# One decoder step on one core: the samples' top-256 as eight rows halved on ScalarE, and six steps beside it

## The chip, the core and the metric

The kernel runs on one core of one Trainium2 chip. The metric is device time in microseconds (us) of one execution, lower is better. TensorE multiplies matrices, VectorE, ScalarE and GpSimd do the elementwise work, SyncE and two others start DMAs. In rows of the trace PE is TensorE's matmul, PEld its weight load, DVE VectorE, ACT ScalarE, POOL GpSimd.

## What is computed

One layer of a hybrid decoder for 1024 prompt tokens and 8 sample tokens, each sample with 1024 cached positions. The reference, cut to what matters here:

```python
score = jnp.einsum('bqh,bqhl->bql', wi, jax.nn.relu(jnp.einsum('bqhd,bld->bqhl', qi, ki)))
score = jnp.where(causal[None], score, -jnp.inf)
_, sel = lax.top_k(score, topk)            # topk = 256
# attention of the 8 heads over the selected keys and values only
a_out = sparse_attention(...) * silu(ga)
# means over windows of 2, 4, 8, 16 tokens, in four groups of 128 channels
d_g = (cs[t + 1] - cs[t + 1 - w]) / min(pos + 1, w) - u
p_out = (d_g @ w_pool[g]) * pool_scale * silu(gp)
y = x + gate * (concat(a_out, p_out) @ w_out)
```

For a prompt token the 256 largest scores are taken among its causal positions; for a sample among its 1024 cached positions and itself.

## The kernel before

Work stands in this order: the input is transposed and normed (to about 64 us), then come projections in chunks of 344 columns, each a sum of three matmuls for each of eight slices of the inner dimension (`products`, fp32 split in an upper and a lower part). The first eight projections (`first_order`: k, qi1, ga0, qi2, ga1, qi3, ga2, v) run beside the indexer of the prompt; the next thirteen (`order`: u0, u1, u2, gp0, u3, gp1, q0, gp2, q1, q2, q3, gp3, ga3) beside all that the change touches; then come attention and the output projection.

The order on TensorE, VectorE and ScalarE is that of the program (`manual_schedule`), so an instruction that waits holds all that stands behind it on its engine. Side work is written as generators in named queues: `beside(queue, gen, rate)` adds one, `project` calls `tick` after every second slice (six matmuls, four times a chunk, twelve times a projection), and a tick advances the head of each queue by `rate` steps, a step being what lies between two `yield`s. `lag(n)` is n empty steps. `drain` runs what is left. Queues: `weights` (loads and splits of the coming projections' weights), `prep`, `score`, `pool`, `win`, `smp`, `top`, `gate`, `stack`.

What the change touches:

- `topk` (L740, queue `top`, rate TOP = 0.5): the 256 largest of each row for the six prompt blocks TB = 7, 6, 5, 4, 3, 2, 128 tokens each, on 128 partitions. Eight halvings of a threshold `t`: the scores under it are counted, by ScalarE (Sign with an accumulator, L759) for blocks 7, 6 and 5, by VectorE (L762) for the others, and VectorE moves all six thresholds (L765 to L769). Then two rounds of MAX8 and MATCH_REPLACE8 (`largest` L793, `mark` L800) pick the last up to 16 of each row exactly. If any row needs more, which a matmul counts (`p_bad`, `tk_bad`), a branch runs thirty more rounds. Last come the masks `amask` (L829).
- `sample_indexer` (L868, queue `smp`, rate 1) gives the samples' scores `s_sc`, 128 partitions x 9 x 8 samples. `sample_topk` (L937, the same queue) searches the 256th score of each sample bit by bit: twice six rounds (`search`), each comparing 504 candidates on VectorE (`s_fl`, L969) and counting over partitions on TensorE (nine matmuls with `ones_b`, `p_cnt`, L955), then the ties by rank (`p_rk`), then the mask `s_m`.
- `windows` (queue `win`): GpSimd's sums over tokens (L1197), VectorE's means (L1203 to L1208), three empty steps (WLAG), ScalarE's upper part `pdh` (L1211), GpSimd's lower part `pdl` (L1213). `take_gp` multiplies these (`ppo`, L1221) and GpSimd multiplies by the gate (L1226).
- `norm_k` (L1025, queue `prep`, beside the first eight projections): after the sum of squares, one empty step between GpSimd's power and the rest on VectorE (L243).
- The first of the thirteen projections, `u0`, takes its PSUM banks from a pool that opens when the indexer's banks are free; `ps_small` is a pool of two banks that `values` (`pvt`) and `history` (`p_hT`) use too.
- `row` takes one of 29 buffers of 1032 fp32 on 128 partitions.

Of the kernel before, what the change touches and what calls it, by code (L numbers as in the profile page):

```python
# [21 lines left out]
TOP = 0.5  # L22
# [5 lines left out]
WLAG = 3  # L28
# [3 lines left out]
LAG = 5  # L32
# [34 lines left out]
def kernel(  # L67
# [634 lines left out]
    def ordered_halves(hi, lo, src, sign):  # L702
        v = src.bitcast(I16).rearrange("p (n t) -> p n t", t=2)
        nc.vector.tensor_copy(hi, v[:, :, 1])
        nc.vector.tensor_copy(lo, v[:, :, 0].bitcast(U16))
        yield
        nc.vector.tensor_scalar(sign, hi, 0.0, -1.0, op0=ALU.is_lt, op1=ALU.mult)
        nc.vector.tensor_tensor(lo, lo, sign.bitcast(U16), op=ALU.bitwise_xor)
        yield
        nc.vector.scalar_tensor_tensor(hi, sign, 0x7FFF, hi, op0=ALU.bitwise_and, op1=ALU.bitwise_xor)  # L710

    TB = (7, 6, 5, 4, 3, 2)
    BY_ACT = (7, 6, 5)
    NT = len(TB)
# [12 lines left out]
    tk_flag = const.tile([P, NT], BF16, name="tk_flag")  # L727
    for i, b in enumerate(TB):
# [7 lines left out]
    def width(i):  # L736
        return (TB[i] + 1) * P

    def topk():
# [13 lines left out]
        nc.vector.tensor_tensor(t, t, tk_mv[:, :, 0], op=ALU.add)  # L753
        for k in range(HALVINGS):
# [12 lines left out]
            nc.vector.scalar_tensor_tensor(tk["d"], tk["keep"], 0.5 if k < HALVINGS - 1 else 0.0, tk_step[:, k],  # L767
                                           op0=ALU.subtract, op1=ALU.mult)
            nc.vector.tensor_tensor(t, t, tk["d"], op=ALU.add)  # L769
            yield  # L770
        for i, b in enumerate(TB):
# [8 lines left out]
            yield  # L780
# [22 lines left out]
        yield  # L803
        for r in range(WINDOW // 8):
            for i in range(NT):
                largest(i)
                yield
            if r == 0:
                pb = ps_side("p_bad", (P, NT))
                mm(pb, ones_b, tk_flag, start=True, stop=True)  # L810
            those(r)
            if r == 0:
                yield
                with nc.allow_low_precision(reason="a count of at most 768"):
# [50 lines left out]

    def s_bc(t):
        return t.unsqueeze(1).to_broadcast([P, 9, B])

    def sample_indexer():
# [54 lines left out]
        def weigh(b):  # L924
# [842 lines left out]
```

## Time and profile before

| | us |
|---|---|
| median of 3 runs (634.39 to 635.96) | 635.41 |
| profiled execution | 634.29 |
| its span, first to last instruction | 632.6 |

| engine | busy us | share of the span | instructions |
|---|---|---|---|
| PE (TensorE matmul) | 603.4 | 95% | 4197 |
| DVE (VectorE) | 391.7 | 62% | 946 |
| ACT (ScalarE) | 292.0 | 46% | 522 |
| POOL (GpSimd) | 237.7 | 38% | 205 |

The thirteen projections stand between 182.8 and 378 us. A row of the trace's timeline reads: start in us, duration, engine, line, operation, output and inputs, tile and type, count, and in brackets the idle time of that engine before it with what ended it. A releaser is inferred from semaphores; the last of several is named. TensorE's matmuls overlap, so their distance from start to start is the time that each costs.

### The profile page before, as it was taken

To read this page: it belongs to the slowest core of one execution; us is meant where nothing else is said; L and a number is where in the kernel's file an instruction comes from. 1 tells how busy PE (TensorE), PEld (TensorE's weight loads), DVE (VectorE), ACT (ScalarE), POOL (GpSimd) and SP (SyncE) were. 2 spreads that over 40 slices of the span, in tenths; PEclk is the share of its full clock that TensorE was granted. 3 is DMA by queue.
4 is the path that set the end of the run, shared out by engine and by line. 5 is a ranking of instruction groups with operands and counts; after the bars stand their busy time and mean duration, and the time that the engine had idled before them with its cause. 6 is when DMAs were issued, how large, how long until landed. Compare 5 with 4: busy or idle time off the path is not lost.

```text
span 632.6 us, 10965 instructions
## 1 busy us (share of the span) xinstructions
PE 603.4 (95%) x4197; PEld 497.7 (79%) x4197; DVE 391.7 (62%) x946; ACT 292.0 (46%) x522; POOL 237.7 (38%) x205
## 2 busy tenths in 40 slices
PE   6899989999989998799999999999999999999997
PEld 5678989999979888789988876566676566878876
DVE  5887365647464788998765337655686765464242
ACT  6635435545456883223223448755787554202000
POOL 3302343211247559674544782502445033106000
PEclk9899998999999999899999999999999999999999
DMA  9994114130427122122543254311221046056232
GB/s 309 286 284 96 51 34 131 46 93 11 122 56 210 50 67 57 48 68 46 133 121 106 88 154 132 127 35 34 68 68 33 2 132 219 19 169 204 96 101 68
DMA packets 75292, 66.05 MB, mean 104 GB/s; under 512 B 21828, under 2 KB 63900, under 8 KB 75229
## 3 DMA queue, kind: packets, MB, share of 16 engines
q1 hardware_dynamic: 69731, 50.57, 28.3%
q0 software_dynamic: 3008, 10.49, 5.6%
q10 hardware_dynamic: 2498, 4.27, 1.8%
q8 instruction: 33, 0.54, 0.4%
q14 instruction: 22, 0.18, 0.1%
HBM read 54.44 MB, written 11.10 MB: 104 GB/s over the span
## 4 chain that ended last, share of the span: by engine, by line
PE 70%; DVE 10%; ACT 5%; SPq 4%; POOL 3%; issue 3%; DMA 3%; POOLq 0%; ACTq 0%; DVEq 0%
PE py L1700 14%; PE po L1616 7%; PE pj_q L515 7%; PE pT L1600 6%; PE pj_ga L515 6%; PE pl L1579 6%; PE pj_gp L515 4%; PE pi L669 4%; PE pj_qi L515 3%; ACT sg L759 3%; SPq L328 2%; PE pj_k L515 2%; PE pj_v L515 2%; SPq L281 2%; DVE sc L779 1%
## 5 line engine op out<-in xcount | busy, mean ns | idle before, releaser
L678 DVE SCALAR_TENSOR_TENSOR sc<-r,wtok,sc 128x512 f32<-128x512 f32 (+5 forms) x42 | 45.1, 1082 | 28.1 <-ACT r L671 26.9
L1588 ACT ACTIVATE pr<-pr,mx,rq 128x128 f32<-128x128 f32 (+7 forms) x64 | 55.4, 866 | 12.3 <-DVE mx L1586 11.8
L671 ACT ACTIVATE r<-pi 128x512 f32<-128x512 f32 (+5 forms) x48 | 36.3, 760 | 53.4 <-PE pi L669 40.7
L1616 PE MATMUL po<-pTs,v_sb 128*64 128x256 f32 (+1 forms) x320 | 52.6, 381 | 0.0
L1700 PE MATMUL py<-woh,mh 128*128 128x512 f32 (+1 forms) x136 | 52.2, 384 | 0.0
L1700 PE MATMUL py<-woh,ml 128*128 128x512 f32 (+1 forms) x136 | 51.8, 381 | 0.0
L1700 PE MATMUL py<-wol,mh 128*128 128x512 f32 (+1 forms) x136 | 51.8, 381 | 0.0
L1600 PE MATMUL pT<-ident,pr 128*128 128x128 f32 x288 | 48.8, 282 | 0.1
L1582 DVE CUSTOM_DVE_ANT_0 pr<-pl,amask 128x384 f32<-128x384 f32 (+5 forms) x48 | 42.1, 885 | 9.3 <-PE pl L1579 8.9
L1600 PEld LDWEIGHTS pT<-ident,pr 128*128 128x128 f32 x288 | 32.5, 141 | 17.5 <-issue 15.6
L146 ACT COPY pTs<-pT 128x512 f32<-128x512 f32 x40 | 23.3, 582 | 33.5 <-PE pT L1600 33.5
L1720 DVE TENSOR_TENSOR y<-py,gate_p 128x512 f32<-128x512 f32 (+1 forms) x17 | 11.2, 657 | 42.6 <-PE py L1700 42.6
L515 PE MATMUL pj_u<-hh,wh_u 128*128 128x344 f32 x96 | 32.3, 337 | 1.7 <-ACT r L671 1.7
L1444 POOL TENSOR_TENSOR wol<-wo,woh 128x1024 fp32r<-128x1024 f32 x8 | 19.5, 2454 | 36.5 <-ACT woh L1443 30.2
L515 PE MATMUL pj_gp<-hh,wh_gp 128*128 128x344 f32 x96 | 33.1, 345 | 0.0
L148 DVE COPY pTs<-pT 128x512 f32<-128x512 f32 (+1 forms) x40 | 23.3, 582 | 15.0 <-PE pT L1600 12.3
L515 PE MATMUL pj_q<-hh,wh_q 128*128 128x344 f32 x96 | 32.2, 335 | 0.0
L515 PE MATMUL pj_ga<-hh,wh_ga 128*128 128x344 f32 x96 | 31.7, 330 | 0.0
L1616 PEld LDWEIGHTS po<-pTs,v_sb 128*64 128x64 f32 x320 | 18.0, 135 | 17.4 <-issue 9.4
L515 PE MATMUL pj_gp<-hl,wh_gp 128*128 128x344 f32 x96 | 31.5, 329 | 0.0
L515 PE MATMUL pj_gp<-hh,wl_gp 128*128 128x344 f32 x96 | 31.4, 327 | 0.0
L515 PE MATMUL pj_ga<-hh,wl_ga 128*128 128x344 f32 x96 | 31.3, 326 | 0.0
(451 smaller groups left out, 1747.5 us busy)
## 6 DMA issues: line engine op xcount, KB each, us to landing
ada<-in_w_ada_dram SPq DMA_DIRECT2D x16, 512.0 KB
x<-in_x_prompt_dram SPq DMA_DIRECT2D x8, 512.0 KB
gate<-in_w_ada_dram SPq DMA_DIRECT2D x8, 512.0 KB
mix<-mix_dram SPq DMA_DIRECT2D x8, 512.0 KB
xr<-in_x_prompt_dram SPq DMA_DIRECT2D x15, 256.0 KB
out_dram<-y ACTq DMA_DIRECT2D x15, 256.0 KB
mix_dram<-sga SPq DMA_DIRECT2D x12, 172.0 KB
mix_dram<-sgp SPq DMA_DIRECT2D x12, 172.0 KB
```

Source lines behind the costliest of these rows:

```text
L146: nc.scalar.copy(out, in_)
L148: nc.vector.tensor_copy(out, in_)
L515: mm(pt[:m, :n], wt[:, k, :m], ht[k][:, c0:c0 + n], start=k == 0 and q == 0, stop=k == KT - 1 and q == 2)
L669: mm(pt[:, c, :n], lhs, kk[:, l0:l0 + n], start=kk is kih, stop=kk is kil)
L671: nc.scalar.activation(r[:, 0:L].rearrange("p (c n) -> p c n", c=nh), pt[:, 0:nh, :n], AF.Relu)
L678: nc.vector.scalar_tensor_tensor(sb[:, 0:L], r[:, 0:L], wtok[:, b, h:h + 1], sb[:, 0:L], op0=ALU.mult, op1=ALU.add)
L1579: mm(pt[:, c, :n], qst[j][s][:, b * P:(b + 1) * P], ksst[s][w][:, l0:l0 + n], start=w == 0, stop=w == 1)
L1582: nc.vector.tensor_tensor_reduce(out=pr[:, 0:L].rearrange("p (c n) -> p c n", c=nh), in0=pt[:, 0:nh, :n], in1=amask[b].rearrange("p (c n) ...
L1588: exps.append(lambda: nc.scalar.activation(pr[:, 0:L], pr[:, 0:L], AF.Exp, scale=sc, bias=mx, accum_out=sums[j, m][:, bq, s:s + 1]))
L1600: nc.tensor.transpose(pt[:, s, bq * P:(bq + 1) * P], probs[j, 2 * m + bq, s][:, k * P:(k + 1) * P], ident)
L1616: mm(po[j, m][64 * s:64 * s + 64, 0, q0:], v_sb[:, k, 64 * s:64 * s + 64], pTs[j, m, k][:, s, q0:], start=k == 0, stop=k == nk - 1)
L1700: mm(pt[:, part], a[k][:, bs], w[:, part], start=k == ks[0] and q == 0, stop=k == ks[-1] and q == 2)
```

## The change

The samples' search is rewritten. The scores of the eight samples are transposed into eight rows of 1025 on eight partitions (`s_row`), and a threshold per row is halved eight times wholly on ScalarE (`half_way`: Sign over the row with the count accumulated, Sign of the limit minus the count, Identity that moves the threshold by a step). Two rounds on VectorE pick the last up to 16, and `sample_masks` transposes the mask back. The six steps beside it: blocks 7 and 6 of the prompt are halved wholly on ScalarE too, and block 5's count goes to VectorE, so that VectorE moves its own four thresholds alone; the steps of `topk` are cut otherwise and run at TOP = 0.57; `topk` waits before its last rounds until the queue `smp` is empty, and the branch serves both; `norm_k` leaves three empty steps in place of one; the means' upper part on ScalarE comes after six empty steps in place of three; `u0` takes its banks from `ps_small`.

```diff
-TOP = 0.5
+TOP = 0.57
-    BY_ACT = (7, 6, 5)
-    NT = len(TB)
+    BY_ACT = (7, 6)
+    NT, NA = len(TB), len(BY_ACT)
...
+    def half_way(sc, t, cnt, lim, sign, step, junk):
+        nc.scalar.activation(junk, sc, AF.Sign, scale=-1.0, bias=t, accum_out=cnt)
+        nc.scalar.activation(sign, cnt, AF.Sign, scale=-1.0, bias=lim)
+        nc.scalar.activation(t, sign, AF.Identity, scale=step, bias=t)
     def topk():
...
+        for k in range(HALVINGS):
+            nc.gpsimd.tensor_scalar(tk_step[:, k, 0:NA], tk_step[:, k, 0:NA], 0.5, None, op0=ALU.mult)
         yield from lag(2)
...
         for k in range(HALVINGS):
-            for i, b in enumerate(TB):
-                L = width(i)
-                if b in BY_ACT:
-                    nc.scalar.activation(junk_tile("sg", tag="junka", bufs=1)[:, :L], score[b], AF.Sign, scale=-1.0,
-                                         bias=t[:, i:i + 1], accum_out=cnt[:, i:i + 1])
-                else:
-                    nc.vector.tensor_scalar(junk_tile("junk")[:, :L], score[b], t[:, i:i + 1], None,
-                                            op0=ALU.is_lt, op1=ALU.add, accum_out=cnt[:, i:i + 1])
-            yield
-            nc.vector.tensor_tensor(tk["keep"], cnt, tk["least"], op=ALU.is_le)
...
+            for i in range(max(NA, NT - NA)):
+                if i < NA:
+                    half_way(score[TB[i]], t[:, i:i + 1], cnt[:, i:i + 1], tk_lim[:, i:i + 1], tk_sign[:, i:i + 1],
+                             tk_step[:, k, i:i + 1], junk_tile("sg", tag="junka", bufs=1)[:, :width(i)])
+                if i < NT - NA:
+                    o = NA + i
+                    nc.vector.tensor_scalar(junk_tile("junk")[:, :width(o)], score[TB[o]], t[:, o:o + 1], None,
+                                            op0=ALU.is_lt, op1=ALU.add, accum_out=cnt[:, o:o + 1])
+                if i % 2:
+                    yield
+            nc.vector.tensor_tensor(tk["keep"][:, by_dve], cnt[:, by_dve], tk["least"][:, by_dve], op=ALU.is_le)
...
+        yield from lag(2)
+        nc.vector.tensor_tensor(t[:, by_act], t[:, by_act], tk_step[:, HALVINGS - 1, by_act], op=ALU.add)
         for i, b in enumerate(TB):
...
-            yield
+            if i < 3:
+                yield
...
+        while queues["smp"]["gens"]:
+            yield
         for r in range(WINDOW // 8):
             for i in range(NT):
                 largest(i)
-                yield
+                if i in (0, 1, 3, 5):
+                    yield
             if r == 0:
-                pb = ps_side("p_bad", (P, NT))
-                mm(pb, ones_b, tk_flag, start=True, stop=True)
+                pb = ps_side("p_bad", (P, NT + 1))
+                mm(pb[:, 0:NT], ones_b, tk_flag, start=True, stop=True)
+                mm(pb[:, NT:], ones_b[0:B, :], s_tk["flag"], start=True, stop=True)
...
                 mark(i)
-                yield
+                if i in (0, 1, 3, 5):
+                    yield
         with tc.If(nc.vector.value_load(tk_bad) != 0, preferred_fallthrough_block=False):
...
+                sample_round(r)
+        yield from sample_masks()
...
-    def sample_topk():
...
+    def sample_round(r):
+        sr = s_row["scores"]
+        sel, off, top = s_tk["sel"][:, 0:8], s_tk["off"][:, 0:8], s_tk["top"]
+        nc.vector.tensor_scalar(sel, tk_order[0:B, 0:8], 8.0 * r, s_tk["need"], op0=ALU.add, op1=ALU.is_lt)
+        nc.vector.tensor_scalar(off, sel, 1.0, -NEG, op0=ALU.subtract, op1=ALU.mult)
+        nc.vector.max(top, sr)
+        nc.vector.tensor_tensor(top, top, sel, op=ALU.mult)
+        nc.vector.tensor_tensor(top, top, off, op=ALU.add)
+        nc.vector.match_replace(sr, top, sr, NEG)
+    def sample_search():
+        sr = s_row["scores"] = row("s_row")[0:B, 0:S + 1]
+        fl = row("s_fl", BF16)[0:B, 0:S + 1]
...
+        for g in range(2):
+            pt = ps_side(f"p_row{g}", (B, 4, P))
+            for i in range(4):
+                nc.tensor.transpose(pt[:, i, :], s_sc[:, 4 * g + i, :], ident)
+            yield
+            nc.vector.tensor_scalar(by_slot(sr)[:, 4 * g:4 * g + 4, :], pt, 0.0, None, op0=ALU.add)
+            yield
+        st = small.tile([P, 6], F32, tag="tk_st", name="s_st")[0:B]
+        nc.vector.bn_stats(st, sr[:, 0:2 * P])
+        nc.vector.bn_aggr(s_tk["mv"], st)
+        yield
+        nc.gpsimd.tensor_tensor(s_tk["sd"], s_tk["mv"][:, 1:2], tk["half"][0:B, 0:1], op=ALU.pow)
+        for k in range(HALVINGS):
+            nc.gpsimd.tensor_scalar(s_tk["step"][:, k:k + 1], s_tk["sd"], spans[7][1] * 2.0 ** -(k + 1), None, op0=ALU.mult)
+        nc.gpsimd.tensor_scalar(t, s_tk["sd"], spans[7][0], s_tk["mv"][:, 0:1], op0=ALU.mult, op1=ALU.add)
+        yield from lag(3)
+        for k in range(HALVINGS):
+            half_way(sr, t, s_tk["cnt"], s_tk["lim"], s_tk["sign"], s_tk["step"][:, k:k + 1], fl)
+            yield
+            yield
+        yield from lag(6)
...
+        nc.vector.tensor_scalar(s_tk["flag"], need, float(WINDOW), None, op0=ALU.is_gt)
+        for r in range(WINDOW // 8):
+            yield
+            sample_round(r)
+    def sample_masks():
+        sr = s_row["scores"]
+        nc.vector.tensor_scalar(sr, sr, TAKEN, MASKED, op0=ALU.is_gt, op1=ALU.mult)
...
+        yield from lag(4)
+        pt = ps_side("p_smask", (P, 8, B))
+        for i in range(8):
+            nc.tensor.transpose(pt[:, i, :], by_slot(sr)[:, i, :], ident[0:B, 0:B])
+        yield
+        nc.vector.tensor_copy(s_m[:, 0:8, :], pt)
+        yield
...
         rest = rstd_of(rs, ss, 2 * nblk, 64, parts=parts)
-        yield
+        yield from lag(3)
         rest()
...
-        yield from lag(WLAG)
+        yield from lag(2 * WLAG)
         nc.scalar.copy(hi, cur)
...
-    beside("smp", sample_topk(), 1.0)
+    beside("smp", sample_search(), 1.0)
...
             u = row(f"u{i}")
-            project(name, CHUNKS, copy_out(u))
+            project(name, CHUNKS, copy_out(u), None if i else ps_small)
...
-    drain("win", "prep", "pool", "top", "smp", "stack")
+    drain("win", "prep", "pool", "smp", "top", "stack")
```

## Rows read from the trace of the kernel before

**Rows 1.** Windows: stretch, its length, busy us (instructions) by engine, clock, DMA share, GB/s.

```profile
64.00:180.90 116.90, 113.83 (x660) 109.33 (x658) 64.42 (x101) 55.81 (x91) 30.95 (x19) 0.99 0.25 66
...
182.80:257.50 74.70, 70.38 (x503) 65.46 (x504) 54.63 (x155) 46.46 (x87) 49.19 (x45) 1.00 0.38 102
257.50:292.60 35.10, 30.39 (x206) 29.62 (x205) 34.03 (x58) 11.13 (x19) 22.87 (x16) 0.90 0.21 48
292.60:378.00 85.40, 84.23 (x659) 75.28 (x657) 46.89 (x132) 29.27 (x56) 50.41 (x25) 1.00 0.37 107
378.00:560.00 182.00, 181.67 (x1321) 117.45 (x1322) 114.54 (x348) 109.04 (x212) 57.08 (x55) 1.00 0.25 82
```

**Rows 2.** Waits of TensorE from 64 to 378 us: total us, times, longest.

```profile
PE p_cnt L955 <- DVE s_fl L969: 5.7, 3, 3.3
...
PE put L1188 <- DVE rx L926: 1.9, 1, 1.9
PE pj_u L515 <- ACT r L671: 1.7, 1, 1.7
PE p_ix L912 <- DVE sx L917: 1.1, 1, 1.1
PE ppo L1221 <- DVE qss L1265: 1.0, 1, 1.0
```

**Rows 3.** Waits of VectorE from 182.8 to 378 us, the longest in total.

```profile
DVE tk_keep L765 <- ACT sg L759: 11.8, 6, 3.4
```

**Rows 4.** Timeline near 95 us, VectorE and TensorE.

```profile
90.33 2.34 DVE L243 TENSOR_TENSOR yt<-y 128x8 f32<-128x8 f32 x1 [1.75 <-POOL y L240]
...
95.52 0.68 PE L669 MATMUL pi<-kih,qis 128*128 128x448 f32 x2 [2.88 <-ACT r L671]
```

**Rows 5.** Timeline from 259 to 270 us, GpSimd, VectorE and TensorE.

```profile
259.72 2.40 POOL L1213 TENSOR_TENSOR pdl<-ps,pdh 128x1032 fp32r<-128x1032 f32 x1 [5.80 <-issue]
...
259.94 2.21 DVE L977 SCALAR_TENSOR_TENSOR s_H<-s_d,s_H 128x8 f32<-128x8 f32 x1
...
264.74 0.58 PE L955 MATMUL p_cnt<-s_fl,ones_b 128*128 128x56 bf16 x9 [3.27 <-DVE s_fl L969]
...
265.56 0.49 PE L515 MATMUL pj_gp<-hl,wh_gp 128*128 128x344 f32 x1
...
269.86 0.49 PE L515 MATMUL pj_gp<-hl,wh_gp 128*128 128x344 f32 x1
```

**Rows 6.** Timeline of TensorE at one count without a wait.

```profile
302.42 0.38 PE L955 MATMUL p_cnt<-s_gt,ones_b 128*128 128x8 bf16 x9
302.66 0.40 PE L515 MATMUL pj_gp<-hh,wh_gp 128*128 128x344 f32 x1
302.90 0.32 PE L515 MATMUL pj_gp<-hl,wh_gp 128*128 128x344 f32 x1
```

**Rows 7.** Chain of work in order of time: start, us, engine, tile, line, count.

```profile
207.45 1.25 ACT sg L759 x2
...
309.27 5.77 PE pj_q L515 x36
```

**Rows 8.** ScalarE's lines 427 and 1588: ns min/median/max, first and last start.

```profile
L427 ACT ACT_TABLE_LOAD  x1: 1283/1283/1283, 1.7 to 1.7; - x1
L427 ACT ACTIVATE warm<-ones_f x1: 202/202/202, 3.0 to 3.0; 128x1 f32<-128x1 f32 x1
...
L1588 ACT ACT_TABLE_LOAD  x1: 1283/1283/1283, 378.5 to 378.5; - x1
```

**Rows 9.** Groups of VectorE, 182.8 to 378 us: count | busy us, mean ns | idle before.

```profile
L800 DVE MATCH_REPLACE8 sc<-tk_top,sc 128x1024 f32<-128x1024 f32 (+5 forms) x12 | 10.4, 873 | 0.0
L793 DVE MAX8 tk_top<-sc 128x8 f32<-128x1024 f32 (+5 forms) x12 | 10.2, 881 | 0.0
```

**Rows 10.** Timeline of GpSimd near 192 us, the steps' power and products.

```profile
191.51 1.36 POOL L747 TENSOR_TENSOR tk_sd<-tk_mv,tk_half 128x6 f32<-128x6 f32 x1
...
193.26 1.87 POOL L750 TENSOR_SCALAR tk_step<-tk_step 128x6 f32<-128x6 f32 x7
```

More of the change, by code (lines that the diff above doesn't have):

```diff
@@ L31 @@
 IXB = 15
-LAG = 5
 SMP = 1.2
@@ L727 @@
     tk_flag = const.tile([P, NT], BF16, name="tk_flag")
+    tk_lim = const.tile([P, NA], F32, name="tk_lim")
+    tk_sign = const.tile([P, NA], F32, name="tk_sign")
+    for i in range(NA):
+        nc.gpsimd.memset(tk_lim[:, i:i + 1], (TB[i] + 1) * P - 2 * TOPK + 0.5)
     for i, b in enumerate(TB):
@@ L813, in topk @@
                 yield
-                with nc.allow_low_precision(reason="a count of at most 768"):
+                with nc.allow_low_precision(reason="a count of at most 776"):
                     nc.vector.tensor_reduce(out=tk_bad, in_=pb[0:1, :], axis=AX.X, op=ALU.add)
@@ new lines @@
+    s_row = {}
+    s_tk = {n: const.tile([B, k], BF16 if n == "flag" else F32, name=f"s_{n}")
+            for n, k in (("t", 1), ("cnt", 1), ("lim", 1), ("sign", 1), ("sd", 1), ("step", HALVINGS), ("mv", 2), ("ngt", 1),
+                         ("d", 1), ("need", 1), ("flag", 1), ("sel", 16), ("off", 16), ("top", 8), ("self", B))}
+    nc.gpsimd.memset(s_tk["lim"], S + 1 - 2 * TOPK + 0.5)
+    nc.gpsimd.tensor_scalar(s_tk["self"], ident[0:B, 0:B], 1.0, -MASKED, op0=ALU.subtract, op1=ALU.mult)
@@ new lines, in by_slot @@
+    def by_slot(r):
+        return r[:, 0:S].rearrange("b (p t) -> b t p", t=8)
+    def sample_round(r):
[7 more added lines that the diff above has]
+        nc.vector.match_replace(sr, top, sr, NEG)
@@ new lines, in sample_search @@
+    def sample_search():
+        sr = s_row["scores"] = row("s_row")[0:B, 0:S + 1]
+        fl = row("s_fl", BF16)[0:B, 0:S + 1]
+        t, d, ngt, need = (s_tk[n] for n in ("t", "d", "ngt", "need"))
+        nc.vector.tensor_reduce(out=d, in_=s_sc[0:B, 8, :], axis=AX.X, op=ALU.max)
+        nc.vector.tensor_scalar(sr[:, S:S + 1], d, 0.0, None, op0=ALU.add)
+        for g in range(2):
+            pt = ps_side(f"p_row{g}", (B, 4, P))
+            for i in range(4):
+                nc.tensor.transpose(pt[:, i, :], s_sc[:, 4 * g + i, :], ident)
+            yield
+            nc.vector.tensor_scalar(by_slot(sr)[:, 4 * g:4 * g + 4, :], pt, 0.0, None, op0=ALU.add)
@@ L1000, in sample_topk @@
             yield
-        p_rk = ps_side("p_rk", (P, 2, B))
-        mm(p_rk[:, 0, :], tri, s_row, start=True, stop=True)
-        mm(p_rk[:, 1, :], ones_b, s_row, start=True, stop=True)
+        st = small.tile([P, 6], F32, tag="tk_st", name="s_st")[0:B]
+        nc.vector.bn_stats(st, sr[:, 0:2 * P])
+        nc.vector.bn_aggr(s_tk["mv"], st)
         yield
-        nc.vector.tensor_tensor(s_m[:, 0, :], p_rk[:, 0, :], s_eq[:, 0, :], op=ALU.add)
-        for t in range(1, 8):
-            nc.vector.tensor_tensor(s_m[:, t, :], s_m[:, t - 1, :], s_eq[:, t, :], op=ALU.add)
@@ new lines, in sample_search @@
+        nc.gpsimd.tensor_scalar(t, s_tk["sd"], spans[7][0], s_tk["mv"][:, 0:1], op0=ALU.mult, op1=ALU.add)
[5 more added lines that the diff above has]
+        yield from lag(6)
+        nc.vector.tensor_tensor(t, t, s_tk["step"][:, HALVINGS - 1:], op=ALU.add)
+        nc.vector.tensor_scalar(fl, sr, t, None, op0=ALU.is_ge, op1=ALU.add, accum_out=ngt)
@@ new lines, in sample_search @@
+        yield
+        nc.vector.tensor_scalar(d, ngt, float(TOPK), NEG, op0=ALU.is_lt, op1=ALU.mult)
+        nc.vector.scalar_tensor_tensor(sr, fl, d, sr, op0=ALU.mult, op1=ALU.add)
+        yield
+        nc.vector.tensor_scalar(d, ngt, float(TOPK), -1.0, op0=ALU.is_lt, op1=ALU.mult)
+        nc.vector.tensor_scalar(need, d, ngt, float(TOPK), op0=ALU.mult, op1=ALU.add)
+        nc.vector.tensor_scalar(s_tk["flag"], need, float(WINDOW), None, op0=ALU.is_gt)
+        for r in range(WINDOW // 8):
+            yield
+            sample_round(r)
@@ new lines, in sample_masks @@
+    def sample_masks():
+        sr = s_row["scores"]
+        nc.vector.tensor_scalar(sr, sr, TAKEN, MASKED, op0=ALU.is_gt, op1=ALU.mult)
+        nc.vector.scalar_tensor_tensor(s_m[0:B, 8, :], ident[0:B, 0:B], sr[:, S:S + 1], s_tk["self"], op0=ALU.mult, op1=ALU.add)
+        yield from lag(4)
[5 more added lines that the diff above has]
+        yield
@@ L1034, in norm_k @@
         rest = rstd_of(rs, ss, 2 * nblk, 64, parts=parts)
-        yield
+        yield from lag(3)
         rest()
```

81 lines of the change are left out of this document (4 added, 77 removed).

## The prediction

> **What bounds the kernel now.** Three views were read, in this order. The busy time by stretch says where TensorE is the bound [rows 1]: from 64 to 181 us it works 113.8 of 116.9 us, from 378 to 560 us it never rests, and between them, in the thirteen projections where the change lies, it works 185.0 of 195.2 us. The one poor stretch is 257.5 to 292.6 us: TensorE 30.4 of 35.1 us, granted clock 0.90, VectorE 34.0 of 35.1 us. So TensorE's instruction stream is the path everywhere, and only its own work or its own waits can be taken out. The waits of TensorE by releaser are the second view [rows 2]: 5.7 us for `s_fl` (samples' search on VectorE), 1.9 and 1.1 us behind small VectorE steps, 1.7 us at the first projection `u0`, 1.0 us behind `qss`. The third view, the timeline, says why VectorE was late in each case.
>
> Two causes are seen. VectorE waits in its fixed order for other engines: 11.8 us in all for ScalarE's Sign counts [rows 3], and 1.75 us for GpSimd's power in `norm_k`, after which its next step lasts 2.34 us; TensorE, waiting for a relu that waits for VectorE's next sum, stands still for 2.88 us until 95.5 us [rows 4]. And VectorE's small steps stretch when GpSimd works: `s_H`, 128x8, took 2.21 us, begun 0.2 us after GpSimd's 2.40 us `pdl` and ended with it; TensorE then stood for 3.27 us at `p_cnt`, and the next projection matmuls follow each other in 0.287 us ((269.86 - 265.56) / 15) [rows 5] where 0.16 us is usual (5.77 / 36) [rows 7]: the lower level of the clock, 1.2 GHz, which returned to 2.4 GHz at 270 us.
>
> Steps are counted in ticks: `project` calls `tick` after every sixth matmul, so thirteen projections are 156 ticks, now 195.2 / 156 = 1.25 us each.
>
> **The change, part by part.**
>
> *Samples' search, TensorE's share.* Fourteen counts over partitions go, 126 matmuls. One set of nine lasts 302.66 - 302.42 = 0.24 us, and the projection matmul behind it 0.24 instead of 0.16 us [rows 6, 7]: 14 x 0.32 = 4.5 us, and the two `p_rk` matmuls about 0.2 us. Added are two groups of four transposes into rows, one of eight back, and one matmul of eight partitions beside `p_bad`. The trace has no such transposes. Four of them lie between a set of `p_cnt` (0.24 us) and four projection matmuls (0.64 us) [rows 6, 7]; taken 0.4 us with the change of operand, near the short end as they have 128 columns where a projection matmul has 344: three groups, 1.2 us. Net gain 3.5 us (bounds 2.8 to 4.0).
>
> *Waits of TensorE for that search.* All 5.7 us on `s_fl` end [rows 2]: no matmul needs a count any more, and the two places where TensorE reads VectorE's sample results (`p_row`, `p_smask`) come two and seven ticks after them. The clock's dip behind the long one cost 15 x (0.287 - 0.16) = 1.9 us in the rows shown and about 0.4 us at its edges: 2.3 us. Both are gained, 8.0 us; a new late step of VectorE could keep some, so 5 to 8.
>
> *VectorE's work.* Some forty short steps go, many of them stretched as in [rows 5]. Added are two sample rounds, each one MAX8 and one MATCH_REPLACE8 over 1025 numbers on eight partitions, priced as the widest of the rows [rows 9] at about 1.2 us each, and a few short ones: 6 us. Block 5's count comes over from ScalarE, eight times about 1 us. VectorE gets lighter, and I count no gain for that beyond the waits named.
>
> *The search on ScalarE.* A halving is the Sign with its accumulator, 1.25 us at 1024 columns [rows 7], and two activations of one column. The only one of that shape took 0.20 us [rows 8]; the new ones have one and two operands from memory, so 0.2 to 0.4 us each, taken 0.3 us. A halving of the samples is 1.85 us, and one comes every second tick, 2.3 us at the expected pace: 80% of ScalarE for 16 ticks. Its other work here (projections' evacuations, one weight copy per projection) needs about a quarter, so ScalarE falls some 1 to 2 us behind. What hides that: the projections' four PSUM banks, three chunks of some 4.6 us ahead. In `topk` ScalarE now does two blocks instead of three, 2 x (1.25 + 0.6) = 3.7 us at most in three steps of 1/0.57 tick, 6 us, where it was three Signs of up to 1.25 us in four ticks, 5 us: lighter. VectorE no longer waits for ScalarE in a halving, which removes the 11.8 us of [rows 3] and with it what stood behind them: the 1.9 us at `put` and 1.1 us at `p_ix` [rows 2]. I take 2.2 of 3.0 us (0 to 3), since GpSimd can still stretch a VectorE step there.
>
> One rule speaks against this edit. ScalarE loaded a function table twice in the whole kernel, at its start and at the first Exp [rows 8], though by the code Sign, Silu and copies alternate on it during `gp0`. The Trainium skill ("ScalarE: Activation LUTs", section "Table sets: the hidden batching unit") says that functions are loaded as sets and that every change of set costs a load, so that calls should be batched by set. By it a search between Silus could cost loads, the second rival below; the trace shows none where Sign and Silu alternate.
>
> *The new order of queues.* `topk` waits until the samples' queue is empty. By the yields that queue ends at tick 85 (before: 143), and `topk` then has 26 steps at 0.57 per tick, to tick 130 (before: 126). Attention needs the masks at tick 156, so 26 ticks, some 30 us, cover this; the branch that skips the exact rounds stays.
>
> *GpSimd.* Samples' steps add one power and nine short operations, and `topk` eight short ones. By the rows 1.36 us and about 0.27 us each (1.87 / 7) [rows 10]: 4.0 + 2.1 us. ScalarE's first sample halving stands behind GpSimd's ten, issued four ticks (4.6 us) earlier: a wait of 0 to 4 us on ScalarE if GpSimd is behind, with the evacuations queued behind it, hidden by the banks.
>
> *Rows.* `s_row` and `s_fl` take two of the 29 buffers in `rows` from tick 51 to 82 and 123. By the code 16 hold h, five the scores, and the pooling sums, means, `u3` and `up_out` the rest; at ticks 66 to 82 I count 30 or 31 wanted. GpSimd's `pdl` of group 2 and the sums of group 3 would wait for group 1's products at tick 73, and ScalarE's `qsq` at 77 for a row. GpSimd has about 14 us of work then and VectorE needs its result at tick 85: just in time.
>
> *`norm_k`.* Its two steps on VectorE are put two ticks apart further. VectorE then has steps of the indexer to do where it waited 1.75 us and was stretched, so the relu's buffers come free some 3 us earlier and the 2.88 us of TensorE end. The granted clock of 0.99 over the 116.9 us [rows 1] leaves room for a dip behind that stop: 1.2 us. Together 4.1 us at most, 0 at least, if another step is stretched there; 3.8 taken, near the top because VectorE's wait is itself removed. The three stores behind these steps and the page numbers come two to six ticks later, past a weight load on SyncE; they are first read at 183 us and later.
>
> *`u0` in the small banks.* It need not wait for the indexer's last banks: 1.7 us [rows 2]. It shares two buffers with `values` and `history`, and its third chunk must wait for ScalarE's copy of the second, 344 columns, by [rows 7] a third of 1.25 us, and the way there: +0.5 us. Gain 1.2 us (0 to 1.7).
>
> *ScalarE's copy of the means* three ticks later, and the loss of the `s_m` steps at the end: the 1.0 us behind `qss` ends; 0.9 us (0 to 1).
>
> *New waits.* From GpSimd, the rows and ScalarE's fuller stretch: 0 to 10 us, taken 2.5 us, because each has a cover of several us.
>
> Sum: 3.5 + 8.0 + 2.2 + 3.8 + 1.2 + 0.9 - 2.5 = 17.1 us. The profiled execution took 634.3 us (span 632.6 us and 1.7 us around it), 1.1 us under the median of 635.4 us. 634.3 - 17.1 = 617.2, on the median's footing 618.3, given as 618. Everything behind 378 us only moves.
>
> **The rivals.**
>
> *GpSimd or the rows give part of it back.* For: GpSimd worked 49.2 of 74.7 and 22.9 of 35.1 us [rows 1]; the second stretch shrinks by some 10 us and gets the samples' operations, and rows are short exactly there. Against: TensorE never waits for GpSimd in [rows 2]. If the sums start only when `s_fl` is freed at tick 82, VectorE is held at tick 85 for some 14 us, TensorE stops about eight ticks later at the q norms, for 5 us, and a clock dip adds 2.3 us: 625.5 us.
>
> *ScalarE reloads its tables* around the three Silu between the samples' halvings: six loads of 1.28 us [rows 8], 7.7 us at most: 626 us. Two loads in the whole kernel speak against it.
>
> *The path is not where I see it* (the gains reappear as waits at other places in the projections, through ScalarE's order): 634 us. For it stands the stretch from 257.5 us, where VectorE is busier than TensorE; against it that this stretch is the one whose VectorE work goes.
>
> *Slower: the exact rounds run.* The branch decides by one count over all prompt and sample rows; it falls when more than 16 scores of any of the eight sample rows are left to find after eight halvings from mean and deviation of 256 of the 1025 scores. Then thirty rounds run: 5.1 us of MAX8, 5.2 us of MATCH_REPLACE8 [rows 9], some 3.3 us for the samples, 30 x 13.6 = 408 us, about 1025 us. Against: the prompt's widest rows use the same halvings from the same starting span and skip the rounds.
>
> **How the numbers follow.** Forecast 618 us with its own range 611 to 624: 0.66. First rival, 624 to 631: 0.17. Tables: 0.01. Better than 611: 0.04. No change: 0.06. Slower: 0.06 (half of it the branch, half an unseen wait). The range 610 to 630 leaves out just under 0.2: no change, slower, the far end of the first rival and most of what is better than 611. About 0.3%, 1.9 us, is what a measurement of this kernel tells from no change: faster 0.88, same 0.06, slower 0.06.
>
> **What would show it.** Right: no TensorE wait for VectorE between 240 and 292 us, the clock at 1.00 there, no 2.88 us wait near 95 us, `u0` right behind the indexer, attention starting near 361 us instead of 378. Wrong: ScalarE idle for GpSimd at the first sample halving, VectorE held at the fourth pooling means, TensorE waiting for banks, or the projections as long as before.

## The result and the profile after

The changed kernel takes 627.05 us (median of 3 runs, 625.83 to 628.07) where the kernel before takes 635.41: a ratio of 0.986 with an interval of 0.984 to 0.988. Measured again beside the experiments it took 626.9 us, ratio 0.984 (0.981 to 0.987). So it is faster, by 8 to 10 us, where 17 were forecast.

By stretch, in answer to the third and fourth line of [rows 1]: length, busy us (instructions) of PE, PEld, DVE, ACT and POOL, clock, DMA share, GB/s.

```profile
257.50:292.60 35.10, 34.02 (x229) 33.10 (x228) 27.36 (x46) 22.30 (x49) 22.64 (x16) 1.00 0.29 66
292.60:370.00 77.40, 71.74 (x502) 63.60 (x501) 40.80 (x89) 28.30 (x54) 48.58 (x24) 1.00 0.38 110
```

The stretch from 257.5 us was mended as meant: VectorE 27.4 us instead of 34.0, ScalarE 22.3 instead of 11.1, TensorE 34.0 instead of 30.4, clock 1.00 instead of 0.90. But from 292.6 us on TensorE now rests 5.7 us, where it rested 1.2. The waits of TensorE from 60 to 375 us, in answer to [rows 2] (total, times, longest; those of 0.2 us left out), say at what:

```profile
PE pg L1518 <- DVE qss L1267: 3.0, 1, 3.0
PE ppo L1223 <- DVE rx L936: 2.0, 1, 2.0
PE ppo L1223 <- DVE qss L1267: 1.9, 1, 1.9
PE pwsb L884 <- DVE wis_bd L881: 1.8, 1, 1.8
PE ppo L1223 <- ACT pt L1226: 1.1, 1, 1.1
PE pj_q L514 <- POOL wl_q L297: 0.5, 1, 0.5
```

Not one wait of [rows 2] is left at its place, and neither is the 2.88 us wait of [rows 4]; six new ones stand there, 10.3 us together. The matmuls `ppo` and `pg` read neither `rx` nor `qss`: by the code they, and before them `put`, take the next of the two PSUM buffers `sm` (`ps_two`), and wait for the step that empties it. Four of the six waits, 8.0 us, are for these two buffers; no run gave them a third. Two places of TensorE split the time: its last `pi` of the indexer (180.48 us before, 177.88 after) and the first `pl` of attention (378.05 and 369.53 us). Up to the first, counted from the first `pj_ki` behind the load of the input (27.38 and 29.76 us, so 2.38 us later after), it is 153.10 us before and 148.12 after: 4.98 us gained. Between the two it is 197.57 and 191.65 us: 5.92 gained. Behind the second nothing moves (254.55 and 254.57). 4.98 + 5.92 - 2.38 is the 8.5 us between the spans, 632.6 and 624.1.

For the projections the balance is this. TensorE's busy time between the two places falls from 185.62 to 181.00 us: 4.6 us, for the matmuls that went (about 3) and the clock dip of [rows 5] (about 2). Its idle time falls from 11.95 only to 10.65 us, 1.3 us: 11.4 us of waits of [rows 2] ended (5.7 + 1.9 + 1.7 + 1.1 + 1.0), and 10.3 us came. 4.6 + 1.3 = 5.9 us. Before, then after:

```profile
180.48:378.05 197.57, 185.62 (x1368) 170.62 (x1366) 137.83 (x345) 88.67 (x164) 123.54 (x85) 0.98 0.34 93
...
177.88:369.53 191.65, 181.00 (x1257) 166.77 (x1255) 132.43 (x299) 103.27 (x212) 123.86 (x103) 1.00 0.35 96
```

Where the new waits come from, first at 243 us. Timeline of VectorE, GpSimd and TensorE there:

```profile
237.83 0.39 DVE L768 TENSOR_TENSOR tk_keep<-tk_cnt,tk_least 128x4 f32<-128x4 f32 x1
238.25 0.85 DVE L770 SCALAR_TENSOR_TENSOR tk_d<-tk_keep,tk_step 128x4 f32<-128x4 f32 x1
239.14 1.82 DVE L772 TENSOR_TENSOR tk_t<-tk_t,tk_d 128x4 f32<-128x4 f32 x1
...
242.73 0.22 DVE L936 SCALAR_TENSOR_TENSOR rx<-p_ixT,wsb 128x64 f32<-128x64 f32 x1
...
235.77 2.43 POOL L1215 TENSOR_TENSOR pdl<-ps,pdh 128x1032 fp32r<-128x1032 f32 x1 [3.52 <-ACT pdh L1213]
238.16 0.93 POOL L1228 TENSOR_TENSOR sgp<-sgp,pt 128x344 f32<-128x344 f32 x1
239.04 1.89 POOL L1199 TENSOR_TENSOR ps<-u 128x1023 f32<-128x1023 f32 x1
...
243.00 0.43 PE L1223 MATMUL ppo<-pdh,wph 128*128 128x344 f32 x1 [2.01 <-DVE rx L936]
```

Three VectorE steps of four columns, 0.15 to 0.17 us when nothing is beside them, take 0.39, 0.85 and 1.82 us, and each ends within 0.05 us of a GpSimd instruction: 238.22 with `pdl` (238.20), 239.10 with `sgp` (239.09), 240.96 with `ps` (240.93). Two counts later comes `rx`, and TensorE waits for it.

The same stretch stands ahead of the 1.9 us at 297 us. VectorE, GpSimd and TensorE:

```profile
285.61 2.44 DVE L958 TENSOR_SCALAR s_off<-s_sel 8x8 f32<-8x8 f32 x1
...
285.64 2.38 POOL L297 TENSOR_TENSOR wl_q<-wr_q,wh_q 128x1024 fp32r<-128x1024 f32 x1
...
297.34 0.40 PE L1223 MATMUL ppo<-pdh,wph 128*128 128x344 f32 x1 [1.95 <-DVE qss L1267]
```

This step of the samples' second round, eight columns on eight partitions, takes 2.44 us and ends with GpSimd's `wl_q` (288.05 and 288.02 us), and `s_sel` ahead of it takes 1.20 us and ends with GpSimd's `ps` (285.58 and 285.56). The same two steps took no more than 0.30 and 0.16 us elsewhere (278.71 us here, "samples later" below). From there to `qss` at 296.96 us VectorE waits for nothing. That the 1.9 us would go without the stretch is argued from these rows; no run tried it.

Second, at 325 us, VectorE and TensorE:

```profile
324.15 0.69 DVE L1006 TENSOR_SCALAR s_row<-s_row 8x1025 f32<-8x1025 f32 x1 [3.79 <-issue]
...
325.02 0.15 DVE L1266 COPY qss<-pqt 128x16 f32<-128x16 f32 x1
...
325.39 0.59 PE L1518 MATMUL pg<-ev_g,fold 128*9 128x256 f32 x2 [3.05 <-DVE qss L1267]
```

The idle 3.79 us, for which no semaphore stands, is the branch, read and skipped; `qss` is queued behind it, and TensorE waits for `qss`. Third, at 181 us (VectorE, then TensorE):

```profile
176.43 5.00 DVE L677 SCALAR_TENSOR_TENSOR sc<-r,wtok,sc 128x1024 f32<-128x1024 f32 x4 [1.06 <-ACT r L670]
...
181.60 0.43 PE L884 MATMUL pwsb<-wis_bd,ones_f 8*128 8x64 f32 x2 [1.77 <-DVE wis_bd L881]
```

`u0` does start right behind the indexer, and runs into VectorE's last four sums: 1.8 us instead of 1.7.

Last, ScalarE's halving of the samples, the first of eight. It holds ScalarE for 1.89 us, to 256.15 us where the next step starts, and 1.85 were forecast; the 1.1 us wait at 269 us is for a `pt` that stands behind the sixth:

```profile
254.26 1.16 ACT L734 ACTIVATE s_fl<-s_row,s_t 8x1025 bf16<-8x1025 f32 x1 [4.42 <-POOL s_t L984]
...
255.53 0.29 ACT L735 ACTIVATE s_sign<-s_cnt,s_lim 8x1 f32<-8x1 f32 x1
255.86 0.39 ACT L736 ACTIVATE s_t<-s_sign,s_t,s_step 8x1 f32<-8x1 f32 x1
```

### The profile page after: what moved, and what is told of

It reads as the page before. It is cut to its first block, busy times and chain, and to the rows that moved or that the text cites. A ratio compares the mean times of both kernels' runs of the same rounds, so it can differ in the third digit from the quotient of the medians.

```text
span 624.1 us, 10765 instructions
## 1 busy us (share of the span) xinstructions
PE 596.9 (96%) x4086; PEld 492.8 (79%) x4086; DVE 386.9 (62%) x900; ACT 306.7 (49%) x570; POOL 238.5 (38%) x226
## 5 line engine op out<-in xcount | busy, mean ns | idle before, releaser
L1591 ACT ACTIVATE pr<-pr,mx,rq 128x128 f32<-128x128 f32 (+7 forms) x64 | 55.4, 866 | 12.3 <-DVE mx L1589 11.8
L514 PE MATMUL pj_gp<-hh,wh_gp 128*128 128x344 f32 x96 | 31.7, 330 | 0.0
L514 PE MATMUL pj_q<-hh,wl_q 128*128 128x344 f32 x96 | 30.8, 321 | 0.5 <-POOL wl_q L297 0.5
L1703 PEld LDWEIGHTS py<-woh,mh 128*128 128x128 f32 x136 | 25.6, 188 | 6.9 <-DVE y L1724 0.8
```

What stands on the lines that cost most here:

```text
L514: mm(pt[:m, :n], wt[:, k, :m], ht[k][:, c0:c0 + n], start=k == 0 and q == 0, stop=k == KT - 1 and q == 2)
L1591: exps.append(lambda: nc.scalar.activation(pr[:, 0:L], pr[:, 0:L], AF.Exp, scale=sc, bias=mx, accum_out=sums[j, m][:, bq, s:s + 1]))
L1703: mm(pt[:, part], a[k][:, bs], w[:, part], start=k == ks[0] and q == 0, stop=k == ks[-1] and q == 2)
```

## The experiments

All numbers are from several executions beside the kernel before on the same chip; ratios are to that. "Projections" is the time from the last `pi` to the first `pl` in the profiled execution, which need not be a typical one.

| kernel | us | ratio (interval) | projections us |
|---|---|---|---|
| before | 635.4 to 636.3 | 1 | 197.6 |
| changed | 626.9 | 0.984 (0.981 to 0.987) | 191.7, 195.1 |
| branch later | 622.1 | 0.978 (0.976 to 0.980) | 189.9 |
| samples later | 621.8 | 0.977 (0.975 to 0.979) | 191.0 |
| `u0` as before | 623.7 | 0.985 (0.981 to 0.989) | 191.0 |
| `norm_k` as before | 632.0 | 0.994 (0.992 to 0.996) | 194.8 |
| samples' search as before | 638.9 | 1.004 (1.002 to 1.006) | 206.8 |
| prompt halving as before | 637.9 | 1.002 (1.000 to 1.005) | 205.6 |
| both searches as before | 642.4 | 1.010 (1.008 to 1.012) | 211.2 |
| one-tensor steps | 627.3 | 0.985 (0.983 to 0.988) | 197.4 |
| before + `norm_k` alone | 632.0 | 0.994 (0.992 to 0.996) | 202.0 |
| samples later, one-tensor steps | 622.9 | 0.980 (0.978 to 0.982) | 189.9 |
| samples and branch later | 619.1 | 0.974 (0.972 to 0.976) | 186.2 |

**The branch.** Two empty steps of `topk` ahead of it:

```diff
+        yield from lag(2)
         with tc.If(nc.vector.value_load(tk_bad) != 0, preferred_fallthrough_block=False):
```

> The changed kernel with two empty steps of topk ahead of the branch. In the changed kernel VectorE reached the branch before the copies qss of the q norms, stood 3.79 us for it, and TensorE stood 3.05 us at pg for the PSUM bank that these copies free. Theory A (late VectorE steps in fixed order): the copies now come first, the wait at pg goes, the total falls by about 3 us, to 624 us on the footing of the median 627.05. Rival B (GpSimd is the next bound and VectorE is behind in any case): the wait at pg shrinks by less than 1 us and the total stays within 1 us of 627.

It took 622.1 us. The wait at `pg` is gone and no other wait grew by more than 0.1 us; the 3.79 us are still there on VectorE, but `qss` now comes ahead of them (320.52 us, the step behind the branch at 324.75). Shown: those 3.0 us were the branch's place in VectorE's order, not its cost. The time fell by more, 4.8 us. On record is the mean granted clock of every execution: the changed kernel takes 623.2 to 625.8 us in the three of its nine executions at 0.997 and 626.9 to 628.1 us in the six at 0.986 to 0.992, while all five of this kernel are at 0.997. At that clock the gain is 2.6 us (621.8 against 624.4 on average); the rest goes with the clock, which dips in most executions of the changed kernel.

**The samples later.**

```diff
     def sample_indexer():
+        yield from lag(2)
         wis_bd = const.tile([B, B, HEADS], F32, name="wis_bd")
```

> The changed kernel with two empty steps at the start of the sample indexer. In the changed kernel the first projection began 4.5 us earlier than before, but TensorE then stood 1.77 us at pwsb for VectorE, which still had four of the indexer's sums to do. Theory A: the gain of the u0 step was only handed on to pwsb; with pwsb later the wait goes and the total falls by about 1.8 us, to 625.3 us. Rival: another step behind the same sums waits in its place, 627 us.

621.8 us. TensorE's waits there:

```profile
PE p_smask L1012 <- DVE s_row L1007: 2.8, 1, 2.8
PE ppo L1224 <- DVE rx L937: 1.9, 1, 1.9
PE p_ix L923 <- DVE rx L937: 1.0, 1, 1.0
```

The 1.8 us at `pwsb` shrink to 0.3, and with them go the waits at `pt`, at the last `ppo` and at `pg`: two ticks change who meets whom. `p_smask` and `p_ix` are new. The 2.8 us at `p_smask` are a stretched step again, with one tensor and constants, 0.69 us in the changed kernel (VectorE and GpSimd):

```profile
323.58 3.49 DVE L1007 TENSOR_SCALAR s_row<-s_row 8x1025 f32<-8x1025 f32 x1 [3.17 <-issue]
...
324.19 2.33 POOL L297 TENSOR_TENSOR wl_gp<-wr_gp,wh_gp 128x1024 fp32r<-128x1024 f32 x1
```

The time fell by more than theory A said (625.3 us).

**`u0` in its old banks.**

```diff
-            project(name, CHUNKS, copy_out(u), None if i else ps_small)
+            project(name, CHUNKS, copy_out(u))
```

> The changed kernel with u0 in its old PSUM banks. Theory A (the gain was handed on to pwsb): the wait returns to the first matmul of u0, about 1.8 us, and the one at pwsb goes; the total stays at 627 us within 1 us. The forecast's own sum: 1.2 us slower, 628.3 us.

One of the six executions took 632.2 us, and the ratio of 0.985 has it in; the other five average 624.2 us, 0.982 of the kernel before. Either way it is that of the changed kernel within the intervals: this step is worth nothing that can be told, since the 1.7 us come back at `pj_u` and the 1.8 us at `pwsb` go. The forecast's own sum, 628.3 us, did not come.

**`norm_k` as before, and alone.**

```diff
-        yield from lag(3)
+        yield
         rest()
```

> The changed kernel with one empty step in norm_k as before. In the changed kernel the indexer ended 2.6 us earlier than before and the 2.88 us wait near 95 us was gone. Theory A: it returns with its dip of the clock, 2.6 to 4 us slower, 630 to 631 us. Rival: the early gain is lost later in any case, because the projections end by something else than TensorE's start: 627 us.

> The kernel before with norm_k's three empty steps alone. Theory A (this step is worth its wait of 2.9 us and the clock dip behind it in either kernel): some 5 us, 630 to 632 us where the kernel before takes 636. Theory B (the time is handed on in the projections, as u0's was): 634 to 636 us, with a larger wait behind 180 us.

Without the step 632.0 us, and `pi` waits again:

```profile
PE pi L668 <- ACT r L670: 3.1, 2, 2.9
```

What the step does is seen in the changed kernel, VectorE, beside [rows 4]:

```profile
90.64 1.01 DVE L677 SCALAR_TENSOR_TENSOR sc<-r,wtok,sc 128x768 f32<-128x768 f32 x1
91.72 0.75 DVE L675 TENSOR_SCALAR sc<-r,wtok 128x1024 f32<-128x1024 f32 x1
93.18 2.35 DVE L242 TENSOR_TENSOR yt<-y 128x8 f32<-128x8 f32 x1 [0.71 <-POOL y L239]
```

Two indexer sums stand ahead of the step on `y`, which is stretched as before and no longer holds the relu's buffers.

With this step alone the kernel before takes 632.0 us, ratio 0.994 (0.992 to 0.996): 3.7 us. Up to the last `pi` both traces say the same, 148.1 us with the step and 152.8 or 153.1 without it, 4.7 to 5.0 us. So in the lone kernel 1.0 to 1.3 us seem to be handed back in the projections. The profile cannot say where: its 202.0 us are those of an execution of 635.5 us, the longest of the twelve, with three clock dips.

**Each search taken back.** The samples' search of before (`sample_topk`, with `topk` not waiting for it); then the prompt rows' halving of before:

```diff
-    beside("smp", sample_search(), 1.0)
+    beside("smp", sample_topk(), 1.0)
```

```diff
-    BY_ACT = (7, 6)
+    BY_ACT = (7, 6, 5)
...
-            nc.vector.tensor_tensor(tk["keep"][:, by_dve], cnt[:, by_dve], tk["least"][:, by_dve], op=ALU.is_le)
+            nc.vector.tensor_tensor(tk["keep"], cnt, tk["least"], op=ALU.is_le)
```

> The changed kernel once more, as the bar for the kernels beside it. Both theories expect the ratio of 0.986 again, 626 to 628 us where the kernel before takes 635.4 to 635.8.

> The changed kernel with the samples' search of before: bit by bit over 128 partitions, counted on TensorE, and topk not waiting for it; the other steps stay. Theory A (the search was worth its 3.5 us of matmuls and its 8.0 us of waits and dip, and what is missing was given back at new waits, of which the rows' late qss, the ScalarE copy pt and the branch, 1.9 + 1.1 + 3.0 us, come with the row search): undoing it costs 11.5 - 6 = 5.5 us, 632 to 633 us against the changed kernel's 627. Theory B (its waits would have shrunk anyhow, because the other steps make VectorE lighter, and only the matmuls were saved): no s_fl wait over 1 us and 630 us or less.

> The changed kernel with the prompt rows' halving of before: three blocks counted on ScalarE, all six thresholds moved by VectorE; the other steps stay. Theory A (VectorE waiting for ScalarE's counts cost TensorE 2.2 us, as forecast): some 10 us of tk_keep waits on VectorE come back and 629 to 631 us. Theory B (those waits were off the path): the VectorE waits come back, and the time stays within 1 us of the changed kernel's 627.

> The changed kernel with both searches of before, the samples' and the prompt rows'; norm_k, u0 and the means' copy stay changed. Each search alone taken back cost 11 to 12 us. Theory A (they need each other: one new search beside one old one leaves VectorE late where the old pair and the new pair do not): 629 to 633 us, under both single ones at 638 to 639. Theory B (each search has a price of its own, and the two add): 627 + 12 + 11 = 650 us.

Neither theory gave the sizes. With the old samples' search 638.9 us, slower than before, and TensorE waits for it longer than ever:

```profile
PE p_cnt L975 <- DVE s_fl L989: 8.8, 3, 4.9
```

With the old prompt halving 637.9 us. Its waits of TensorE, and VectorE and GpSimd at the longest:

```profile
PE p_ix L916 <- DVE sx L921: 4.0, 1, 4.0
PE p_ix L916 <- DVE tk_d L766: 2.7, 1, 2.7
```

```profile
223.18 3.37 DVE L764 TENSOR_TENSOR tk_keep<-tk_cnt,tk_least 128x6 f32<-128x6 f32 x1 [2.31 <-ACT sg L758]
...
226.79 1.86 DVE L768 TENSOR_TENSOR tk_t<-tk_t,tk_d 128x6 f32<-128x6 f32 x1
228.57 0.28 DVE L921 COPY sx<-p_ix 128x128 f32<-128x128 f32 x1
...
222.25 2.43 POOL L1209 TENSOR_TENSOR pdl<-ps,pdh 128x1032 fp32r<-128x1032 f32 x1
224.65 1.88 POOL L1193 TENSOR_TENSOR ps<-u 128x1023 f32<-128x1023 f32 x1
...
226.74 1.89 POOL L1193 TENSOR_TENSOR ps<-ps 128x1022 f32<-128x1022 f32 x1
```

VectorE waits 2.31 us for ScalarE's count, its step then stands 3.37 us through the rest of `pdl` and the whole of `ps`, a third one 1.86 us through the next `ps`: 7.8 us from 220.86 to 228.65 us with almost no work done, and `sx`, for which TensorE waits 4.0 us, is behind it.

Both searches old take 642.4 us, ratio 1.010. By the ratios, of 636 us: the new samples' search is worth 4.6 us beside the old prompt halving and 12.7 us beside the new one; the new prompt halving 3.7 us beside the old samples and 11.8 us beside the new. So at this pace (0.57) they do support each other, by 8 us. But the pair of old ones with `norm_k`, `u0`, the later means and the recut `topk` at 0.57 is 10 us slower than the kernel before with `norm_k` alone (642.4 against 632.0): the forecast of theory A, that the old pair would be as good as before, fell. The rows point at `topk`'s faster pace, which fits the new halving only: `p_ix` waits 4.0 and 2.7 us with the old pair too, where it waited 1.1 us in [rows 2]. The pace was not tried by itself, so that stays an inference.

**One tensor for each step.** Does GpSimd slow every small VectorE step, or only those that read two tensors? The three steps of four columns, two SBUF tensors each, are written as eight of one column, each with one tensor and scalars:

```diff
-            nc.vector.tensor_tensor(tk["keep"][:, by_dve], cnt[:, by_dve], tk["least"][:, by_dve], op=ALU.is_le)
...
+            for o in range(NA, NT):
+                one = slice(o, o + 1)
+                nc.vector.tensor_scalar(tk["keep"][:, one], cnt[:, one], float(width(o) - TOPK), tk_step[:, k, one],
+                                        op0=ALU.is_le, op1=ALU.mult)
...
+                    nc.vector.tensor_scalar(t[:, one], t[:, one], tk["keep"][:, one], tk_step[:, k + 1, one],
+                                            op0=ALU.add, op1=ALU.subtract)
```

> The changed kernel with the three 128x4 threshold steps of VectorE, which read two tensors from SBUF each, written as eight 128x1 steps that read one tensor and scalars. Theory A (a VectorE step with two SBUF operands stands until GpSimd's two-operand instruction ends, others don't): each new step takes 0.1 to 0.3 us whatever GpSimd does, against up to 2.35 us; the 2.0 us wait of TensorE at ppo <- rx near 243 us ends, and the time is 624 to 626 us. Theory B (GpSimd slows every small step of VectorE): new steps of 1 to 2.4 us are seen, the wait stays, 627 to 629 us.

The groups of the new steps, ns min/median/max and first and last start, then VectorE and GpSimd at the place shown above:

```profile
L771 DVE TENSOR_SCALAR tk_keep<-tk_cnt,tk_step x32: 192/204/210, 193.2 to 242.7; 128x1 f32<-128x1 f32 x32
...
L778 DVE TENSOR_SCALAR tk_t<-tk_t,tk_keep,tk_step x28: 258/265/268, 193.7 to 238.6; 128x1 f32<-128x1 f32 x28
```

```profile
238.04 0.81 DVE L778 TENSOR_SCALAR tk_t<-tk_t,tk_keep,tk_step 128x1 f32<-128x1 f32 x4
...
238.15 1.89 POOL L1206 TENSOR_TENSOR ps<-u 128x1023 f32<-128x1023 f32 x1
```

None of the 60 is stretched, with GpSimd at the same work beside them, and the 2.0 us at `rx` are gone: shown is that GpSimd's stretch of these steps made that wait. But theory A's rule, that only steps with two SBUF tensors stretch, fell: `s_off`, 8x8, one tensor and constants, takes 2.45 us in this kernel too, as in the changed one above. One column was free of it, eight were not. And the time is 627.3 us, so theory A's price did not come either. The wait at `pt` grows from 1.1 to 2.4 us, and the rows on the way there are these (GpSimd, VectorE, ScalarE):

```profile
247.98 1.19 POOL L1207 COPY ps<-ps 128x4 f32<-128x4 f32 x1
...
247.69 1.43 DVE L791 SCALAR_TENSOR_TENSOR sc<-fl,tk_d,sc 128x1024 f32<-128x1024 bf16 x1
...
253.79 1.16 ACT L734 ACTIVATE s_fl<-s_row,s_t 8x1025 bf16<-8x1025 f32 x1 [6.19 <-POOL s_t L991]
```

GpSimd's copy of four columns, 0.19 us in the changed kernel, ends with a two-tensor step of VectorE: GpSimd is held by VectorE too. ScalarE waits 6.19 us for `s_t` instead of 4.42 and starts its samples 78.3 us behind the last `pi` instead of 76.4 (253.79 - 175.53 and 254.26 - 177.88), and `pt` stands behind them. Clock dips in that profile cost another 4.7 us, counted from projection matmuls at 0.29 instead of 0.16 us.

**Together.** Samples later with `p_smask` two steps later, and the one-tensor steps; then samples and branch later; both with TOP = 0.62, so that the masks are done in time.

> The changed kernel with the samples' indexer two steps later, p_smask two steps later, TOP 0.62, and VectorE's threshold steps on one tensor each. Theory A (each wait left has a cause of its own and goes with it): the waits at rx, branch and p_smask, 2.0, 2.8 and 2.8 us in the runs before, all end: 617 to 619 us. Theory B (VectorE's lateness is handed on to the next reader): other waits of 3 to 5 us in all come, 621 to 624 us.

> The changed kernel with the samples' indexer two steps later, two empty steps ahead of the branch and TOP 0.62. Theory A (the gains of the two single runs, 4.9 and 5.2 us, come from different waits and add in part): 618 to 620 us. Theory B (both freed the same wait behind the branch, and the rest is handed on): 621 to 623 us.

622.9 and 619.1 us. In the first the `rx` and `p_smask` waits end and the branch's 3.3 us are back: theory B. The second is the best of all, 16 us under the kernel before, with these waits of TensorE:

```profile
PE ppo L1225 <- DVE qss L1269: 1.4, 1, 1.4
PE ppo L1225 <- DVE rx L938: 1.3, 1, 1.3
PE p_ix L924 <- DVE tk_keep L768: 1.1, 1, 1.1
PE p_ix L924 <- DVE sx L929: 0.8, 1, 0.8
```

With 0.3 us at `pwsb` 4.9 us instead of 10.3, and the projections are shorter by 5.4 us than in the first profile of the changed kernel (186.2 against 191.7 us, both at clock 1.00). So most of what the forecast missed was in these waits, and could be had by moving two steps and setting the pace; the share of each of the three is not told apart.

## Why the prediction was right or wrong

The direction held, and the range of 610 to 630 us by the room left in it for rivals: 627 us lies outside the forecast's own 611 to 624. The gain of 17.1 us was twice what came. Step by step:

- *TensorE's share of the samples' search*, 3.5 us: nearly right. The two `p_row` groups cost 0.7 us in all, `p_smask` about 1.0 where a group was put at 0.4; about 3 us are left.
- *Its waits*, 8.0 us: the rows behaved as said. No matmul waits for a count, and the first profile has no dip between 240 and 292 us. But in the second profile of the same kernel, with dips behind the `pwsb`, `rx` and `pg` waits, TensorE was busy 5.3 us longer (186.3 against 181.0): the new stops can bring a dip each, though they need not. The 2.3 us for the dip were safe only if nothing took the old wait's place.
- *`put` and `p_ix`*, 2.2 us: both waits ended and the 11.8 us of [rows 3] with them, and `ppo` <- `rx` took 2.0 us in their place. The sentence that GpSimd "can still stretch a VectorE step there" was right, and priced at 0.8 us; at `rx` alone it cost 2.0.
- *`norm_k`*, 3.8 us: right, 3.7 us alone; in the traces 4.7 to 5.0. The mechanism was right by half: VectorE's wait is 0.71 us instead of 1.75, but the step behind it still lasts 2.35 us; it is moved behind two sums, not shortened.
- *`u0`*, 1.2 us: wrong, 0. The step failed where it asked only what TensorE waits for. VectorE's last four sums end 5.0 us after their first starts, and `wis_bd`, which the next matmul `pwsb` reads, stands behind them. [Rows 2] name only the wait that was seen, not the next one in line.
- *The means' copy and the end*, 0.9 us: the 1.0 us behind `qss` ended there, and `qss` returned twice elsewhere, 1.9 and 3.0 us.
- *New waits*, -2.5 us with 0 to 10 as bounds: this is the term that failed. It was 10.3 us. "Each has a cover of several us" was said of GpSimd, the rows and ScalarE. For the projections' own evacuations on ScalarE it held. But the projections' banks that were the cover do nothing for `pt`, which empties an `sm` buffer and stands behind halvings that began after 4.42 us of waiting for GpSimd: 1.1 us, and 2.4 us where that wait was 6.19. GpSimd's late `wl_q` cost 0.5. VectorE's order was not gone through again, and it made 8.7 of the 10.3 us, in part because GpSimd stretches its steps. The branch above all was counted as a question of whether it is taken; that VectorE idles some 3 us when it is skipped stands in the trace of before, and what is queued behind it at its new place was not asked. In the kernel before:

```profile
334.90 3.43 DVE L829 TENSOR_SCALAR amask<-sc 128x1024 bf16<-128x1024 f32 x2 [3.14 <-issue]
```

- *The rivals.* "GpSimd or the rows" gave 625.5 us, the nearest in time. Its mechanism did not happen, so that this is near is luck: VectorE was not held by rows, and GpSimd's part is the stretched steps, 2.0 us at `rx` and, as argued, the 1.9 us at 297 us. "The path is not where I see it" is the better description: about half the gain reappeared as other waits, through VectorE's order and not ScalarE's. The tables were loaded twice, as before. The exact rounds were skipped.
- *The signs.* Of those for right, the wait near 95 us went, the clock was 1.00 and `u0` came right behind the indexer; but TensorE did wait for VectorE between 240 and 292 us (`rx`), and attention started at 369.5 us, not 361. Of those for wrong, two came: ScalarE idle for GpSimd at the first sample halving, and TensorE waiting for banks, the two `sm` buffers.
- *A sum.* GpSimd's operations for the samples were added up as 4.0 us where the rows named give 1.36 + 9 x 0.27 = 3.8; they took 0.58 + 2.87 + 0.26 = 3.7 us. No term rests on it.

Of the stretched steps the forecast said only that GpSimd's work stretches them. The Trainium skill ("SBUF — State Buffer", section "SBUF: two separate sides") gives the rule behind it: VectorE and GpSimd share one pair of SBUF ports, a VectorE instruction with two SBUF inputs or in a two-port mode needs it, and who comes first holds it for a whole instruction. The runs here agree: the stretched steps with two tensors in SBUF end with the GpSimd instruction, the 60 one-column steps with one tensor never stretch, and neither does `rx`, 0.22 us, one of whose inputs is in PSUM. `s_off`, with one tensor, does stretch (2.44 us); whether it ran in a two-port mode no row shows.

## What to carry to other kernels

Where TensorE stops for an engine that works in a fixed order, a removed wait uncovers the next late result in that order: before counting the gain, go through what the slow engine does in the following microseconds and name its next reader and the buffer that it must empty. Steps fitted to each other (a pace, a split, an order) must be priced together: here, at the new pace, each search alone was worth 4 to 5 us beside the other's old form and 12 beside its new one. After such a change look again at where unavoidable idle time lies, like a skipped branch; moving two steps here, with the pace to suit, brought 6.5 to 8 us more, nearly as much as the change itself.

## What was not expected of the hardware

- A skipped branch keeps VectorE idle for 3.0 to 3.9 us ("issue" in the rows) in all profiles here, at its old place and at the new one.
- A small VectorE step can stand through two GpSimd instructions in a row: 3.37 us for 128x6. Steps with one tensor can be held too: 2.44 us for 8x8, 3.49 us for 8x1025.
- One-column activations, taken at 0.3 us each, cost 0.29 us with one operand from memory and 0.39 us with two, where the one with none took 0.20 [rows 8].
- The same kernel in two profiles took 191.7 and 195.1 us for the projections: TensorE was busy 5.3 us longer in the second and waited 1.9 us less (the wait at `pt` is gone there). The clock was granted at 1.00 throughout in the first, as shown at the top, and in the second:

```profile
175.60:370.67 195.07, 186.30 (x1256) 171.55 (x1255) 130.14 (x299) 103.52 (x212) 123.84 (x103) 0.97 0.34 94
```

- The first projection matmul behind the input's load starts between 27.2 and 29.8 us in these profiles, whatever the kernel: a single span says no more than that of a gain.
